# A hybrid encoder layer: gate-weighted one-hots and the forget gate move to ScalarE, one product of the expert search moves to VectorE in 16 bits, and the row fetches get a fifth slot and a wider spacing

## The chip, the core and the metric

The kernel runs on one core of one Trainium2 chip. The metric is the device time of one execution in microseconds (us). The engines are TensorE (PE in the profile; PEld is its weight load), VectorE (DVE), ScalarE (ACT), GpSimd (POOL) and SyncE (SP), each with a queue of its own that runs in order; 16 DMA engines move data between HBM and SBUF.

## What is computed

One layer over 1024 tokens of width 1024: a mixer, and a feed-forward part that picks single-neuron experts.

```python
h    = rmsnorm(x, norm_mix_g)
proj = h @ w_in                                   # q, forget, i, out gate, conv B/C/h, two merge gates
forget = lb + (1 - lb) * sigmoid(hf);  k = 1 - forget;  log_f = log(forget)
y_a  = gated_norm(hgrn2_chunkwise(q, k, log_f, i)) # recurrence in chunks of 64 tokens, 8 heads
y_b  = cb * causal_depthwise_conv(cc * ch, conv_w)
x    = x + (sig(g_a) * (y_a @ w_branch_hg) + sig(g_b) * (y_b @ w_branch_conv)) @ w_out
# experts: 8 heads, 128 x 128 product keys, 16 picks a head
h2   = rmsnorm(x, norm_ffn_g)
s1, s2 = scores of the 128 first and the 128 second keys;  top 16 of each
top_s, pos = top_k(v1[:, None] + v2[None, :], 16);  idx = cand_i[pos];  gate = softmax(top_s)
x    = x + sum over the 128 picks of gate * gelu(peer_u[idx] . h2) * peer_v[idx]
out  = rmsnorm(x, norm_final_g)
```

## The kernel before

The 1024 tokens are 8 tiles of 128. The kernel has two stages.

The **mixer stage** works through five groups of tokens (128, 128, 256, 256, 256). For a group, `front` normalizes and transposes, `recurrence` (L554) makes the gates and runs the chunks, `gates_b` and `gates_a` make the merge gates, and `post` (L603) multiplies by the branch and output matrices, adds the residual, normalizes again and finds the top 16 keys of each head. `picks_of` then runs `pick` (L817) for each tile: 50 candidate sums a head, their top 16, and the number of the expert behind each. For that last step a head compares 16 positions with 50 candidate places on VectorE (L860, 16 x 50 = 800 elements), multiplies the result with the candidates' numbers on GpSimd (L862) and sums on VectorE (L863).

What is done with the picks depends on the tile. Tiles 0, 1, 6 and 7 go **by rows** (`gather`, L895): for each of a token's 128 picks an indirect DMA of GpSimd (L905) fetches one 4 KB row of table U per token, VectorE multiplies it with h2 and sums (L935); 32 picks later the same is done with the rows of table V (L941, into the output). The rows lie in a ring of slots; a slot is fetched anew when the product that reads it is done. Tiles 2 to 5 go **densely**: `all_gates` (L960) writes, for each token, a 128 x 128 table of gates to HBM (the tile wd), and the second stage applies all 16384 experts to those 512 tokens. For the gates, keys and gates of a tile are transposed on PE (L881) and copied out (L887, L889, L890); then, 8 tokens at a time, VectorE makes one-hots of both keys (L998) and multiplies one of them by the gate, in an upper and a lower half of 16 bits (L1002); PE multiplies the two (L979) and ScalarE copies the result out (L983). There are 64 such steps of 8 tokens, 16 a tile.

The **dense stage** (`dense`, L1013) begins when the gates are complete: per block of 128 experts it splits weights into two halves (L238), projects (L286, L289), applies gelu (L1031) and the gates (L1033), and multiplies with V (L1058, L1069). Rows of tiles 6 and 7, and the picks of these tiles, are laid between its steps by `interleave` (L415). At the end come the sums with the residual (L1117) and the final norms.

The order of the mixer stage is set by a planner, `together` (L386). It keeps a clock of PE work, takes of all running pieces the one that is least far behind its budget, and lets it run to its next `yield`; a number that is yielded is a pause on that clock. `PICK` is the pause between the end of a search and the transposes of its keys, `SPREAD` that between making one-hots and multiplying them, and `ROW_STEP` that between two row steps in `paced` (L372); a row step is two rows of U and two of V. Tiles 0 and 1 need 136 row steps. Each engine then works in this order, as a scheduler of the framework puts it.

## Time and profile before

| | us |
|---|---|
| median of 3 runs (lowest, highest) | 3249.61 (3244.61, 3250.73) |
| the profiled execution | 3238.13 |
| its span, first to last instruction | 3236.4 |
| busy: PE / DVE / ACT / POOL | 2830.8 / 2677.1 / 1075.6 / 1577.1 |
| DMA | 979.05 MB, mean 303 GB/s |
| mean granted TensorE clock | 0.927 of full speed |

The mixer stage fills the span up to about 1790 us, the dense stage from there to about 3190; the final 49 us hold norms and the last rows. Busy shares are averages over these stages and say little by themselves. A wait is put down to what ended it last.

### The profile page before, as it was taken

Reading aid. Unit: us, or ns where it says so; the run is one execution under the profiler, and the core shown is the slowest. Engines: PE = TensorE matmul, PEld = TensorE weight load, DVE = VectorE, ACT = ScalarE, POOL = GpSimd, SP = SyncE. Lnnn points to the kernel's source line nnn. Section 1 sums busy time; section 2 is a strip of 40 time slices with the busy share of each in tenths; the row PEclk is TensorE's granted clock in tenths of the full one; section 3 lists DMA queues with packets and bytes.
Section 4 is the critical chain, followed back from the end, with each engine's and each line's share of the span. In section 5 each row is a group of like instructions: output and inputs, shape, how many; then the busy total and the mean of one; then the engine's idle time right before and its main releaser. Section 6 shows DMA issues by size and latency. Waiting matters only on the chain.

```text
span 3236.4 us, 45285 instructions
## 1 busy us (share of the span) xinstructions
PE 2830.8 (87%) x15988; PEld 2434.0 (75%) x15988; DVE 2677.1 (83%) x5673; ACT 1075.6 (33%) x1686; POOL 1577.1 (49%) x1392
## 2 busy tenths in 40 slices
...
GB/s 284 190 273 242 270 316 321 318 273 331 316 305 306 237 288 310 324 299 276 292 304 264 257 283 344 340 351 312 355 314 349 315 355 324 349 319 343 330 328 195
DMA packets 336131, 979.05 MB, mean 303 GB/s; under 512 B 30880, under 2 KB 107168, under 8 KB 333856
## 3 DMA queue, kind: packets, MB, share of 16 engines
...
q8 instruction: 126, 2.06, 0.2%
q14 instruction: 101, 0.83, 0.1%
...
## 4 chain that ended last, share of the span: by engine, by line
PE 56%; DVE 23%; DMA 9%; issue 5%; ACT 3%; POOL 3%; SPq 0%; DVEq 0%; POOLq 0%; ACTq 0%
PE ps L1058 15%; PE ps L286 14%; PE ps L250 10%; PE ps L289 7%; DVE mem_g L941 5%; DMA mem_g<-in_peer_u,idx 4%; DVE mem_g L935 4%; DMA mem_g<-in_peer_v,idx 4%; PE ps L277 2%; PE ps L278 2%; PE ps L279 2%; PE ps L736 1%; DMA mem_z<-in_keys 1%; DVE mem_z L863 1%; DVE mem_y L1002 1%
## 5 line engine op out<-in xcount | busy, mean ns | idle before, releaser
L250 PE MATMUL ps<-mem_h,mem_w 128*128 128x256 f32 (+1 forms) x4480 | 856.8, 350 | 10.4 <-ACT mem_h L260 8.7
L250 PEld LDWEIGHTS ps<-mem_h,mem_w 128*128 128x128 f32 x4480 | 743.4, 200 | 88.0 <-ACT mem_h L260 10.2
L905 POOL DMA_INDIRECT mem_g<-in_peer_u,idx x384 | 486.6, 1267 | 503.6 <-DVE mem_g L935 305.1
L905 POOL DMA_INDIRECT mem_g<-in_peer_v,idx x368 | 450.8, 1225 | 442.2 <-DVE mem_g L941 202.2
L1058 PE MATMUL ps<-mem_v,mem_ph 128*128 128x512 f32 x2304 | 552.2, 390 | 0.5 <-ACT mem_v L237 0.5
L941 DVE SCALAR_TENSOR_TENSOR mem_g<-mem_g 128x1024 f32<-128x1024 f32 x368 | 494.9, 1345 | 50.3 <-DMA mem_g<-in_peer_v,idx 50.0
L935 DVE SCALAR_TENSOR_TENSOR mem_g<-mem_g 128x1024 f32<-128x1024 f32 x384 | 487.1, 1272 | 38.4 <-DMA mem_g<-in_peer_u,idx 37.6
L286 PE MATMUL ps<-mem_ht,mem_s 128*128 128x512 f32 x2048 | 510.6, 392 | 7.0 <-DVE mem_z L1069 4.3
L1058 PEld LDWEIGHTS ps<-mem_v,mem_ph 128*128 128x128 f32 x2304 | 432.6, 188 | 90.4 <-ACT mem_v L237 0.9
L286 PEld LDWEIGHTS ps<-mem_ht,mem_s 128*128 128x128 f32 x2048 | 387.0, 189 | 88.9 <-DVE mem_z L1069 4.9
L237 ACT ACTIVATE mem_s<-mem_raw 128x512 fp32r<-128x512 f32 x256 | 161.2, 631 | 573.3 <-PE ps L286 559.0
L905 POOL DMA_INDIRECT mem_e<-in_peer_u,idx x128 | 186.4, 1456 | 220.9 <-DVE mem_e L935 192.4
L289 PE MATMUL ps<-mem_ht,mem_s 128*128 128x512 f32 x1024 | 275.2, 391 | 0.0
L238 DVE TENSOR_TENSOR mem_s<-mem_raw,mem_s 128x512 fp32r<-128x512 f32 x256 | 177.1, 700 | 110.1 <-PE ps L289 73.2
L905 POOL DMA_INDIRECT mem_e<-in_peer_v,idx x144 | 173.3, 1203 | 139.9 <-DVE mem_g L941 94.0
L289 PEld LDWEIGHTS ps<-mem_ht,mem_s 128*128 128x128 f32 x1024 | 193.4, 189 | 40.3
L941 DVE SCALAR_TENSOR_TENSOR mem_g<-mem_e,mem_g 128x1024 f32<-128x1024 f32 x144 | 184.3, 1280 | 1.3 <-DMA mem_g<-x2d 1.1
L237 ACT ACTIVATE mem_v<-mem_z 128x1024 fp32r<-128x1024 f32 x128 | 128.9, 1053 | 156.7 <-PE ps L279 156.3
L701 POOL TENSOR_TENSOR mem_y<-mem_y 128x128 f32<-128x128 f32 (+1 forms) x120 | 60.1, 501 | 233.4 <-DVE mem_y L570 233.3
L983 ACT COPY mem_a<-ps 128x512 f32<-128x512 f32 x128 | 124.3, 1086 | 140.2 <-PE ps L979 71.2
L862 POOL TENSOR_TENSOR mem_z<-mem_z 128x800 f32<-128x800 f16 x64 | 125.2, 1956 | 86.7 <-DVE mem_z L860 76.0
L935 DVE SCALAR_TENSOR_TENSOR mem_e<-mem_e,mem_g 128x1024 f32<-128x1024 f32 x128 | 156.7, 1230 | 1.5 <-DMA mem_e<-in_peer_u,idx 1.5
(189 smaller groups left out, 3975.9 us busy)
## 6 DMA issues: line engine op xcount, KB each, us to landing
mem_w<-in_w_in SPq DMA_DIRECT2D x200, 512.0 KB, 5.3
mem_raw<-in_peer_ut SPq DMA_DIRECT2D x128, 512.0 KB, 6.8
mem_z<-in_peer_v SPq DMA_DIRECT2D x128, 512.0 KB, 7.8
...
```

The source lines that it names most:

```text
L237: self.nc.scalar.activation(hi, src, AF.Copy)
L238: self.nc.vector.tensor_tensor(lo, src, hi.bitcast(F32), op=ALU.subtract)
L250: self.nc.tensor.matmul(ps, w[:, kk, :], act[:, kk, :], start=kk == 0, stop=kk == k - 1)
L277: mm(ps, lh, rh, start=first, stop=False, **kw)
L286: mm(ps, w[kk][0], act[part][:, kk, :], start=kk == part == 0, stop=False)
L289: mm(ps, w[j][1], act[0][:, j, :], start=False, stop=j == k - 1)
L862: nc.gpsimd.tensor_tensor(pr, eq, ci[:, hd:hd + 1, :].broadcast_to([P, TOPK, NCAND]), op=ALU.mult)
L905: nc.gpsimd.indirect_dma_start(out=r, out_offset=None, in_=a[table], in_offset=bass.IndirectOffsetOnAxis(ap=self.idx[t][:, k:k + 1], axis=0))
L935: nc.vector.scalar_tensor_tensor(u, u, 1.0, h2, op0=ALU.mult, op1=ALU.mult, accum_out=wt[:, k:k + 1])
L941: nc.vector.scalar_tensor_tensor(acc, v, wt[:, k:k + 1], acc, op0=ALU.mult, op1=ALU.add)
L983: nc.scalar.copy(dst[:, :, 4 * h:4 * h + 4].rearrange("p a t -> p t a"), ps.rearrange("p (t a) -> p t a", t=4))
L1058: nc.tensor.matmul(acc[t][hf], pp[c][i][:, tk], vp[c][:, k, 512 * hf:512 * hf + 512], start=c == 0 and i == 0 and k == 0, stop=c == NKEYS ...
```

## The change

Four edits, and three numbers of the planner.

- `all_gates`: the product of the one-hot with the gate leaves VectorE. In place of one instruction of 2048 elements (L1002) ScalarE does 16 activations of 128 elements, each with the token's gate half as its scale, one value per partition. The gate halves are kept as [2, 128] in 32 bits for it, so `pick` copies them out in another way (one more copy on ScalarE, a narrower subtraction on VectorE). The one-hots have two buffers and not three.
- `recurrence`: forget = lb + (1 - lb) * sigmoid and k = 1 - forget leave VectorE (L567, L568) and become two activations with scale and bias.
- `pick`: the product with the candidates' numbers (L862) leaves GpSimd for VectorE; one-hot, numbers and product are unsigned 16-bit integers, which takes one more cast of 400 elements a tile.
- The ring of row slots in the mixer stage has five slots of 4 KB (the fifth is the buffer that the one-hots gave up). The dense stage has eight, as before.
- `ROW_STEP` 6.2 to 7.0, `PICK` 31.25 to 50, `SPREAD` 1.296 to 2.592.

```diff
@@ constants @@
-T_SOON, T_ROWS, ROW_STEP = 300.0, 1e4, 6.2
+T_SOON, T_ROWS, ROW_STEP = 300.0, 1e4, 7.0
...
-LEV, GRAM, STATE, MERGE, NORM, PICK, SPREAD, OUT = 11.55, 1.944, 0.864, 4.752, 3.24, 31.25, 1.296, 3.24
+LEV, GRAM, STATE, MERGE, NORM, PICK, SPREAD, OUT = 11.55, 1.944, 0.864, 4.752, 3.24, 50.0, 2.592, 3.24
@@ place, place_picks, place_dense, schedule @@
-        M.o, M.q = r((80, 84, 220), 4), r((56, 60), 4)
+        M.o, M.q = r((80, 84), 4), r((56, 60), 4)
...
-        M.pr, M.fi, M.ci = r(at + 4, 3.25), r(at + 4, 1), r(at + 7.25, 1.625)
+        M.pr, M.cu, M.fi, M.ci = r(at + 4, 1.625), r(at + 5.625, 1), r(at + 4, 1), r(at + 7.25, 1.625)
...
-        M.rows = (80, 84, 216, 220)
+        M.rows = (80, 84, 216)
...
-        self.rows = self.ring(300, 4, 4)
+        self.rows = self.ring((300, 304, 308, 312, 220), 4)
@@ constants() @@
+        self.one = c.tile([P, 1], F32, tag="one", name="one")
+        nc.vector.memset(self.one, 1.0)
@@ recurrence @@
             nc.scalar.activation(fg, fp[:, :n], AF.Sigmoid)
-            nc.vector.tensor_scalar(fg, fg, self.oml[:, p:p + 1], self.lb[:, p:p + 1], op0=ALU.mult, op1=ALU.add)
-            nc.vector.tensor_scalar(k, fg, -1.0, 1.0, op0=ALU.mult, op1=ALU.add)
+            nc.scalar.activation(fg, fg, AF.Identity, bias=self.lb[:, p:p + 1], scale=self.oml[:, p:p + 1])
+            nc.scalar.activation(k, fg, AF.Identity, bias=self.one, scale=-1.0)
             nc.scalar.activation(fg, fg, AF.Ln)
@@ pick @@
+        cu = mem.cu.take([HEADS, NCAND], U16)
+        nc.vector.tensor_copy(cu, ci)
...
         for hd in range(HEADS):
-            eq, pr = mem.eq.take([TOPK, NCAND], F16), mem.pr.take([TOPK, NCAND])
+            eq, pr = mem.eq.take([TOPK, NCAND], U16), mem.pr.take([TOPK, NCAND], U16)
             nc.vector.tensor_tensor(eq.rearrange("p k (c d) -> p k c d", d=2), ix,
                                     pf[:, hd].unsqueeze(2).broadcast_to([P, TOPK, NCAND // 2, 2]), op=ALU.is_equal)
-            nc.gpsimd.tensor_tensor(pr, eq, ci[:, hd:hd + 1, :].broadcast_to([P, TOPK, NCAND]), op=ALU.mult)
+            nc.vector.tensor_tensor(pr, eq, cu[:, hd:hd + 1, :].broadcast_to([P, TOPK, NCAND]), op=ALU.mult)
             nc.vector.tensor_reduce(xf[:, hd, :], pr, axis=AX.X, op=ALU.add)
...
-        pairs = ps[:, 2 * P:3 * P].unsqueeze(2).broadcast_to([P, P, 2])
-        nc.scalar.copy(gates[:, :, 0, :], pairs)
-        nc.vector.tensor_tensor(gates[:, :, 1, :], pairs, gates[:, :, 0, :], op=ALU.subtract)
+        upper = self.small.tile([P, P], F16, tag="upper", name="upper", bufs=1)
+        nc.scalar.copy(upper, ps[:, 2 * P:3 * P])
+        nc.scalar.copy(gates[:, 0], ps[:, 2 * P:3 * P])
+        nc.vector.tensor_tensor(gates[:, 1], ps[:, 2 * P:3 * P], upper, op=ALU.subtract)
@@ all_gates @@
                     nc.vector.tensor_tensor(o.rearrange("p t i (k d) -> p (t i) k d", d=2), ix,
                                             keys.rearrange("p t i d -> p (t i) d").unsqueeze(2)
                                             .broadcast_to([P, 2 * T, NKEYS // 2, 2]), op=ALU.is_equal)
-                    first = o[:, :, 1, :].rearrange("p t (k d) -> p t k d", d=2)
-                    nc.vector.tensor_tensor(q.rearrange("p t i (k d) -> p t i k d", d=2),
-                                            first.unsqueeze(2).broadcast_to([P, T, 2, NKEYS // 2, 2]),
-                                            gates.unsqueeze(3).broadcast_to([P, T, 2, NKEYS // 2, 2]), op=ALU.mult)
                     yield SPREAD if todo else 0
+                    for tk in range(T):
+                        for i in range(2):
+                            nc.scalar.activation(q[:, tk, i, :], o[:, tk, 1, :], AF.Copy, scale=gates[:, i, tk:tk + 1])
```

How the order of the engines moves at three places. Line numbers of the change are higher by 3 to 7.

PE before, where the last group's recurrence ends: L250 with `mem_yy` is the branch product of `post`, L881 the transposes of tile 4's keys, L979 the one-hot products.

```order
L765 MATMUL ps<-mem_y 64x64 x4
L784 MATMUL ps<-mem_y,c_headmean 128x256
L250 MATMUL ps<-mem_h_157,mem_w 128x256 x32
L250 MATMUL ps<-mem_yy,mem_w 128x256 x32
L881 MATMUL ps<-c_ident,mem_z 128x128 x3
L979 LDWEIGHTS mem_o
L979 MATMUL ps<-mem_y,mem_o 128x128
```

PE with the change, at the same place (L886 are the transposes, L632 is the output projection of `post`, L629 before):

```order
L768 MATMUL ps<-mem_y 64x64 x4
L787 MATMUL ps<-mem_y,c_headmean 128x256
L251 MATMUL ps<-mem_h_159,mem_w 128x256 x32
L251 MATMUL ps<-mem_yy,mem_w 128x256 x32
L632 MATMUL ps<-mem_w,mem_h_159 128x256 x32
L886 MATMUL ps<-c_ident,mem_z 128x128 x3
L986 LDWEIGHTS mem_o
L986 MATMUL ps<-mem_y,mem_o 128x128
```

All 32 products of the first half of the output projection have moved ahead of the transposes.

ScalarE before, from the copies of tile 4's keys and gates on (L887, L889): L983 copies tables of gates out, L847 is the exponential of tile 5's gates, L230 the square sum of the last group's second norm.

```order
L887 CAST mem_z<-ps 128x128x2 x2
L889 CAST mem_z<-ps 128x128x2
L983 COPY mem_a<-ps 128x4x128 x2
L847 ACT_TABLE_LOAD
L847 ACTIVATE mem_z<-mem_z 128x128
L983 COPY mem_a<-ps 128x4x128 x8
L230 ACTIVATE junk,ms<-mem_z 128x1024
L983 COPY mem_a<-ps 128x4x128 x2
L230 ACTIVATE junk,ms<-mem_z 128x1024
```

ScalarE with the change, right behind the copies of tile 4's keys and gates (L990 copies tables out, L850 is the exponential, L231 the square sum, L1012 are the new activations):

```order
L990 COPY mem_a<-ps 128x4x128 x2
L850 ACT_TABLE_LOAD
L850 ACTIVATE mem_z<-mem_z 128x128
L1012 ACTIVATE mem_y<-mem_o,mem_z 128x128 x37
L990 COPY mem_a<-ps 128x4x128 x2
L1012 ACTIVATE mem_y<-mem_o,mem_z 128x128 x11
L990 COPY mem_a<-ps 128x4x128 x2
L231 ACTIVATE junk,ms<-mem_z 128x1024
L990 COPY mem_a<-ps 128x4x128
L1012 ACTIVATE mem_y<-mem_o,mem_z 128x128 x16
L990 COPY mem_a<-ps 128x4x128
L231 ACTIVATE junk,ms<-mem_z 128x1024
```

The two square sums now stand behind 48 and 64 of the new activations.

VectorE before, one head of tile 4's search (L860 compares, L863 sums; between them GpSimd multiplies; L611 is the branch product's gating in `post`):

```order
L863 TENSOR_REDUCE mem_z<-mem_z 128x16
L860 TENSOR_TENSOR mem_z<-iota_x,mem_z 128x800
L935 SCALAR_TENSOR_TENSOR mem_g<-mem_g 128x1024
L611 TENSOR_TENSOR mem_z<-mem_z,ps 128x256
L941 SCALAR_TENSOR_TENSOR mem_g<-mem_g 128x1024
L611 TENSOR_TENSOR mem_z<-mem_z,ps 128x256
L935 SCALAR_TENSOR_TENSOR mem_g<-mem_g 128x1024
L863 TENSOR_REDUCE mem_z<-mem_z 128x16
```

VectorE with the change, one head of the same search (L865 compares, L867 multiplies, L868 sums; L942 and L948 are row products, `mem_a` holds the fifth slot):

```order
L868 TENSOR_REDUCE mem_z<-mem_z 128x16
L865 TENSOR_TENSOR mem_z<-iota_x,mem_z 128x800
L948 SCALAR_TENSOR_TENSOR mem_g<-mem_a,mem_g 128x1024
L867 TENSOR_TENSOR mem_z<-mem_z 128x800
L942 SCALAR_TENSOR_TENSOR mem_g<-mem_g 128x1024
L868 TENSOR_REDUCE mem_z<-mem_z 128x16
```

The product stands between compare and sum on the same engine.

## Rows read from the trace of the kernel before

**Rows 1.** The windows of the profiled execution, by stretch: start and end in us from the span's start, length, then busy us (instructions) of each engine, the granted clock of TensorE as a share of full speed, the busy share of the DMA engines, and GB/s. Picks stand for the search of each token's 128 experts; tiles 2 and 3 are searched from about 1000, tiles 4 and 5 from about 1450, tiles 6 and 7 from about 1750.

```profile
300.00:1050.00 750.00, 665.43 (x4190) 584.54 (x4188) 599.96 (x1589) 233.60 (x404) 388.36 (x415) 0.92 0.87 308
1050.00:1512.00 462.00, 352.93 (x2361) 306.27 (x2361) 421.91 (x1060) 171.74 (x251) 256.38 (x221) 0.87 0.81 285
1512.00:1600.00 88.00, 38.80 (x227) 33.77 (x227) 81.81 (x133) 17.57 (x23) 53.66 (x36) 0.69 0.83 296
1600.00:1800.00 200.00, 125.71 (x848) 111.38 (x849) 190.39 (x511) 77.51 (x111) 100.85 (x69) 0.76 0.85 298
1800.00:3188.00 1388.00, 1383.27 (x6090) 1144.91 (x6090) 1206.01 (x1692) 442.86 (x648) 723.32 (x541) 1.00 0.90 323
3188.00:3237.00 49.00, 2.49 (x11) 1.71 (x10) 42.48 (x89) 5.75 (x10) 15.95 (x14) 0.55 0.58 214
```

**Rows 2.** Who waited for whom from 1050 to 1800: engine, tile and line that waited, what it waited for, us in total, times, longest.

```profile
PE ps L881 <- DVE mem_z L877: 131.3, 4, 48.0
PE ps L979 <- DVE mem_y L1002: 69.0, 13, 21.0
```

**Rows 3.** The timeline of PE around the key transposes of tiles 4 and 5: start us, length us, instruction, and in brackets the idle time before it and what ended it.

```profile
1451.13 12.79 PE L250 MATMUL ps<-mem_yy,mem_w 128*128 128x256 f32 x58 [0.55 <-DVE mem_yy L796]
1511.96 0.90 PE L881 MATMUL ps<-c_ident,mem_z 128*128 128x128 f32 x3 [48.04 <-DVE mem_z L877]
...
1600.25 0.88 PE L881 MATMUL ps<-c_ident,mem_z 128*128 128x128 f32 x3 [45.67 <-DVE mem_z L877]
```

**Rows 4.** Groups of VectorE up to 1870 us, one shape each: line, operation, output<-input, shapes, count | busy us, mean ns of one | idle us before them and what ended it. The picture of what the change takes off VectorE and of the nearest relatives of what it puts there.

```profile
L1002 DVE TENSOR_TENSOR mem_y<-mem_o,mem_z 128x2048 f16<-128x2048 f16 x43 | 57.0, 1327 | 0.5 <-PE ps L979 0.4
L1002 DVE TENSOR_TENSOR mem_y<-mem_a,mem_z 128x2048 f16<-128x2048 f16 x21 | 26.0, 1237 | 0.0
L567 DVE TENSOR_SCALAR mem_y<-mem_y,oml,lb 128x256 f32<-128x256 f32 x12 | 6.4, 531 | 1.8 <-ACT mem_y L566 1.8
L567 DVE TENSOR_SCALAR mem_y<-mem_y,oml,lb 128x128 f32<-128x128 f32 x8 | 2.8, 346 | 4.0 <-ACT mem_y L566 4.0
L568 DVE TENSOR_SCALAR mem_y<-mem_y 128x256 f32<-128x256 f32 x12 | 3.5, 290 | 0.1
L568 DVE TENSOR_SCALAR mem_y<-mem_y 128x128 f32<-128x128 f32 x8 | 1.8, 222 | 0.1
L860 DVE TENSOR_TENSOR mem_z<-iota_x,mem_z 128x800 f16<-128x800 f16 x64 | 36.4, 569 | 0.0
L863 DVE TENSOR_REDUCE mem_z<-mem_z 128x16 f32<-128x800 f32 x63 | 61.5, 976 | 12.7 <-POOL mem_z L862 12.6
```

**Rows 5.** The row products of VectorE (L935 with the row of table U, L941 with that of V), same columns: two groups up to 1870 us, two groups from 1870 us on, and two from 1448 to 1512 us, where tile 4 is searched.

```profile
L935 DVE SCALAR_TENSOR_TENSOR mem_g<-mem_g 128x1024 f32<-128x1024 f32 x256 | 331.9, 1299 | 38.3 <-DMA mem_g<-in_peer_u,idx 37.6
L941 DVE SCALAR_TENSOR_TENSOR mem_g<-mem_g 128x1024 f32<-128x1024 f32 x224 | 310.5, 1386 | 50.1 <-DMA mem_g<-in_peer_v,idx 50.0
...
L941 DVE SCALAR_TENSOR_TENSOR mem_g<-mem_g 128x1024 f32<-128x1024 f32 x144 | 184.4, 1281 | 0.2
L935 DVE SCALAR_TENSOR_TENSOR mem_e<-mem_e,mem_g 128x1024 f32<-128x1024 f32 x128 | 156.7, 1230 | 1.5 <-DMA mem_e<-in_peer_u,idx 1.5
...
L941 DVE SCALAR_TENSOR_TENSOR mem_g<-mem_g 128x1024 f32<-128x1024 f32 x11 | 19.3, 1758 | 2.4 <-DMA mem_g<-in_peer_v,idx 2.4
L935 DVE SCALAR_TENSOR_TENSOR mem_g<-mem_g 128x1024 f32<-128x1024 f32 x11 | 18.3, 1662 | 2.6 <-DMA mem_g<-in_peer_u,idx 2.6
```

**Rows 6.** The product of the search on GpSimd up to 1870 us, same columns.

```profile
L862 POOL TENSOR_TENSOR mem_z<-mem_z 128x800 f32<-128x800 f16 x63 | 123.2, 1955 | 84.6 <-DVE mem_z L860 74.0 <-DVE rs_t L219 4.6 <-DVE mem_y L754 3.3
```

**Rows 7.** The timeline of VectorE and GpSimd in the search of tile 4.

```profile
1493.09 1.27 DVE L941 SCALAR_TENSOR_TENSOR mem_g<-mem_g 128x1024 f32<-128x1024 f32 x1
1494.00 1.85 POOL L862 TENSOR_TENSOR mem_z<-mem_z 128x800 f32<-128x800 f16 x1
1494.29 2.64 DVE L935 SCALAR_TENSOR_TENSOR mem_g<-mem_g 128x1024 f32<-128x1024 f32 x1
```

**Rows 8.** Groups of ScalarE up to 1870 us, one shape each, same columns.

```profile
L983 ACT COPY mem_a<-ps 128x512 f32<-128x512 f32 x128 | 124.3, 1086 | 140.2 <-PE ps L979 71.2 <-DMA wd<-mem_a 57.0 <-DVE mem_g L935 11.1
L517 ACT ACTIVATE mem_a<-mem_a,c_convw 128x256 f32<-128x256 f32 x12 | 6.1, 507 | 92.0 <-DVE mem_a L512 91.9
L517 ACT ACTIVATE mem_a<-mem_a,c_convw 128x128 f32<-128x128 f32 x8 | 3.2, 401 | 12.5 <-DVE mem_a L512 12.5
L789 ACT ACTIVATE mem_y<-mem_y 128x128 f32<-128x128 f32 x8 | 2.5, 309 | 0.3
L569 ACT ACTIVATE mem_y<-mem_y 128x256 f32<-128x256 f32 x12 | 5.0, 417 | 16.3 <-DVE mem_y L568 16.3
```

**Rows 9.** The timeline of ScalarE at two activations that follow each other without a wait.

```profile
1224.73 0.42 ACT L708 ACTIVATE mem_y<-mem_y 128x256 f32<-128x256 f32 x1
1225.05 0.19 ACT L710 ACTIVATE el<-mem_y 128x4 f32<-128x4 f32 x1
```

**Rows 10.** The timeline of VectorE at the end: the last sum with a PSUM bank, the first and the last two of the 22 row products that follow it, and the last instruction.

```profile
3187.12 1.28 DVE L1069 TENSOR_TENSOR mem_z<-mem_z,ps 128x512 f32<-128x512 f32 x2 [4.03 <-PE ps L279]
...
3196.38 1.28 DVE L941 SCALAR_TENSOR_TENSOR mem_g<-mem_g 128x1024 f32<-128x1024 f32 x1
...
3225.17 2.61 DVE L941 SCALAR_TENSOR_TENSOR mem_g<-mem_e,mem_g 128x1024 f32<-128x1024 f32 x2
...
3231.18 1.28 DVE L956 SCALAR_TENSOR_TENSOR mem_g<-mem_g,rstd,mem_e 128x1024 f32<-128x1024 f32 x1
```

More of the change, by code (lines that the diff above doesn't have):

```diff
@@ L15 @@
 I32 = mybir.dt.int32
+U16 = mybir.dt.uint16
 U32 = mybir.dt.uint32
@@ L46 @@
 NCAND = int(sum(NB))
-ITEM = {F32: 4, F32R: 4, U32: 4, I32: 4, F16: 2, BF16: 2}
+ITEM = {F32: 4, F32R: 4, U32: 4, I32: 4, U16: 2, F16: 2, BF16: 2}
 ALWAYS = {"z": (112, 163.5), "g": (300, 325)}
```

8 lines of the change are left out of this document (5 added, 3 removed).

## The prediction, on record before the change was run

> **What bounds the kernel now.** I read the windows by stretch first [rows 1]. From 1800 to 3188 us PE is busy 1383 of 1388 us at a granted clock of 1.00 while VectorE is busy 87%: that stage is PE's. From 1600 to 1800 VectorE is busy 190 of 200 us and PE 126; from 1050 to 1600 VectorE is busy 504 of 550 us (422 and 82) and PE 392. These two stretches are VectorE's, although PE has the larger share over the whole span. From 300 to 1050 nobody is: PE 665, VectorE 600 of 750, the DMA engines at 87%. ScalarE is busy 38% (172, 18 and 78 of 750 us) from 1050 to 1800. Then the waits: PE waits 131.3 us in four waits for the keys of the dense tiles, and 69.0 us for the gate-weighted one-hots [rows 2]; the timeline shows two of the former, 48.04 and 45.67 us, with PE's queue behind them [rows 3]. While PE waits there VectorE works, so such a wait is mostly a sign of VectorE's backlog, and only worth what VectorE can do sooner. At the end, the last PSUM sums start at 3187, and 22 products with V rows run from 3196 to 3228 with the last norms between them [rows 10].
>
> **What VectorE loses and gains.** The gate products take 57.0 + 26.0 = 83.0 us in 64 instructions, the forget gate 6.4 + 2.8 + 3.5 + 1.8 = 14.5 us in 40 [rows 4]. Both go. What comes is 64 products of 800 elements. No row shows one in unsigned 16 bits; nearest is the comparison L860, two 16-bit inputs and as many elements, at 569 ns: 36.4 us. The upper end is the sum L863, which reads 800 elements in 976 ns: 62.5 us. Eight casts of 400 elements lie between L568's 290 ns and L860's 569: about 0.42 each, 3.4 us. The narrower subtraction of the gates is worth under 1 us. Net **-58 us** (-32 if the product is slow).
>
> To this come stalls. In the search of tile 4 the row products take 1758 and 1662 ns, in the dense stage 1281 and 1230 [rows 5]: 11 x 0.48 + 11 x 0.43 = 10 us lost beside the 8 products that GpSimd makes there, so 1.25 us a product in row products alone. The timeline shows one: alone L941 takes 1.27 us; an L935 that starts at 1494.29, 0.29 us after a GpSimd product of 1.85, takes 2.64 and ends 1.1 us after it [rows 7]. Bounds are 0 and the whole 1.955 us of a product [rows 6]; I take 1.0, nearer to the counted rows: **64 us** over all tiles. By the Trainium skill's page "SBUF — State Buffer" (SBUF: two separate sides) a GpSimd operation and a VectorE one with two SBUF inputs lock each other out of a port pair for the whole instruction; the row agrees in kind, and by that page VectorE would get back 125 us, not 64. VectorE's own waits for GpSimd's product, 12.6 us [rows 4], go too.
>
> Row products: the wider step moves none out of the mixer stage (254 and 219 stand ahead of the first dense gating before, 256 and 224 now), only later in it. Ahead of tile 2's keys stand 255 before and 233 now; ahead of tile 5's, 414 and 401; behind those, up to the dense stage, 59 and 79.
>
> **What ScalarE gains.** 1024 activations of 128 elements with a scale read per partition. Nearest is L517 of that shape: 401 ns, against 309 for L789 without such a scale [rows 8]. Neighbours that need not wait overlap: L710 starts at 1225.05, L708 ends at 1225.15 [rows 9]. So 0.30 us from start to start, 307 us in all; the ends are 0.21 (309 less the overlap) and 0.40 (no overlap), 215 and 410. The forget gate adds 12 x 2 x 0.507 + 8 x 2 x 0.401 = 18.6 us by L517's rows; in return ScalarE no longer waits 16.3 us for L568 [rows 8].
>
> **Stretch by stretch**, against the profiled execution of 3238.1 us (span 3236.4), which lies 11.5 under the median of the runs.
>
> - 300 to 1050: 22 row products fewer (27 us) and some 12 us of forget gates less; 24 heads of products more (13.7), 24 us of stalls less: VectorE -49. PE and DMA are near their own ends here, so I take a third: **-15**, with 0 and -45 as ends.
> - 1050 to 1600: 39 gate products less (50 us), 3 of forget gates; 24 heads more (13.7), 24 us of stalls and some 8 of the 12.6 of waits less; 9 row products more (11). VectorE -60 of 504. But ScalarE goes from 189 to about 400 us: 672 activations (204), six table copies more. In a stretch of under 500 us that is over 80%, in order. Half the projection is now ahead of tile 4's transposes on PE, which helps; both square sums of the last norm stand behind 48 to 64 activations on ScalarE, which hurts. I take about 60%: **-37**, ends +15 and -65.
> - 1600 to 1800: 25 gate products less (32 us) and 6 us of stalls; 20 row products more (25) and 8 heads (4.6): VectorE -8. ScalarE: 352 activations (106) more, six table copies (6.5) less, 78 to 177 us of 200. **0**, ends +25 and -15.
> - 1800 to 3188: PE's, the same instructions: **0**.
> - The end: fewer idle row steps (135 steps are placed in the mixer stage, all of use; 139 before, three of which found no picks) leave 14 row products behind the last PSUM sum, not 22. 31.4 us for 22 with the norms between [rows 10] is 1.4 each; 8 fewer is 11, less a little for norms without cover: **-10**.
>
> Sum -62: the profiled execution would be 3176, the median 3249.6 - 62 = **3188 us**. This case takes in 3155 to 3220.
>
> **Rivals.**
>
> 1. *ScalarE's queue becomes the pace* (slower). In the new order the activations stand in 93 blocks, and behind 59 of them something other than a table copy follows directly: a step of the recurrence, a query's copy, a norm. A block of 16 is 4.8 us and itself waits for its one-hot from VectorE, with two buffers in place of three. At half a block each, 59 waits are 142 us; half of it on the path, 71 us, takes the place of the 37 gained from 1050 to 1600: 3249.6 - 25 + 34 = 3259. It decides once waits on the path exceed 62 us. For it: 400 us of work in under 500; 0.40 a piece would make that 465. Against it: ScalarE idled most of the stretch [rows 1]. The Trainium skill's page "ScalarE: Activation LUTs" (Rules for kernel authors) says to multiply on VectorE and not on ScalarE, and speaks against this edit; here the engine that it would spare is the one with time left. Chance 0.15.
> 2. *The relief is not passed on.* PE, the DMA engines or row fetches fill what VectorE leaves; rows already cost it 37.6 + 50.0 us of waits [rows 5]. Only the end's 10 us show: 3240. Against: VectorE was busy 95% ahead of the dense stage. Chance 0.15.
> 3. *All of it counts.* -45, -65, -15 and -10: 3115. It needs ScalarE to be nowhere late. Chance 0.10.
> 4. *The product does not run at 16-bit speed*, 976 ns and not 569: 26 us back, some 16 of them on the path: 3204. Chance 0.10.
>
> The forecast keeps 0.50. Range **3135 to 3262**: it takes in the forecast, rivals 2 and 4, half of rival 1 and part of rival 3; left out are the far ends of 1 and 3. A measurement of this kernel tells some 0.2% (6.5 us) from no change. Faster by more: 0.50 + 0.10 + 0.10 and over half of rival 2, 0.78; within it: the rest of rival 2, 0.07; slower: rival 1, 0.15.
>
> **What would show it.** Right: L941 and L935 near 1281 and 1230 ns in the searches; the stretch in which PE is always busy beginning some 50 us earlier than 1800; PE's waits for the keys well under 131 us; the new activations about 0.30 apart; 14 row products at the end. Wrong: VectorE idle for ScalarE between 1050 and 1800, a product near 976 ns, or an unmoved start of the dense stage.

## The result: 0.8% faster, where 1.9% was forecast

The changed kernel takes **3224.74 us**, the median of 4 runs (3220.0 to 3228.39), the kernel before 3250.17 beside it: ratio 0.9919, 95% interval 0.9893 to 0.9946. That is 25 us less, outside what measurement can take for no change; the forecast was 62 less. Its profiled execution took 3228.39 us, with a span of 3226.6. One run of the experiment e13 below, at 4212.51 us and a granted clock of 0.642, is left out of its median.

Lines have moved: the product is now L867, the comparison L865, the sum L868, the new activations L1012, the one-hot products on PE L986, the key transposes L886, the row products L942 (table U) and L948 (table V), the dense V products L1065 and L278 to L280 (before L1058 and L277 to L279).

The windows after, over the stretches of [rows 1]:

```profile
300.00:1050.00 750.00, 680.28 (x4226) 596.27 (x4225) 567.65 (x1656) 249.24 (x429) 364.16 (x386) 0.92 0.83 300
...
1050.00:1512.00 462.00, 381.58 (x2393) 319.54 (x2392) 386.16 (x975) 307.97 (x765) 226.50 (x220) 0.88 0.85 309
1512.00:1600.00 88.00, 64.03 (x394) 52.03 (x393) 81.16 (x194) 75.51 (x213) 38.13 (x30) 0.83 0.90 328
...
1600.00:1800.00 200.00, 142.16 (x679) 96.31 (x678) 178.61 (x549) 171.40 (x453) 83.69 (x64) 0.72 0.83 296
1800.00:3188.00 1388.00, 1388.00 (x6029) 1130.37 (x6028) 1178.77 (x1591) 433.49 (x633) 704.04 (x530) 1.00 0.88 320
...
3188.00:3237.00 49.00, 1.43 (x7) 0.81 (x5) 32.65 (x79) 5.04 (x10) 7.67 (x6) 0.64 0.35 129
```

From 1050 to 1600 VectorE (the third pair) is busy 36 us less (467 against 504; the forecast had 60 less) and ScalarE (the fourth) 194 more (the forecast had some 210). PE is busy all of 1800 to 3188, as before, and yet does not get through: it runs 6029 instructions where it ran 6090.

The groups of VectorE up to 1870 us and over the whole span (the 16-bit ones), and the new one of ScalarE:

```profile
L942 DVE SCALAR_TENSOR_TENSOR mem_g<-mem_g 128x1024 f32<-128x1024 f32 x206 | 257.2, 1252 | 25.4 <-DMA mem_g<-in_peer_u,idx 23.1 <-issue 1.7
L948 DVE SCALAR_TENSOR_TENSOR mem_g<-mem_g 128x1024 f32<-128x1024 f32 x183 | 239.2, 1307 | 22.6 <-DMA mem_g<-in_peer_v,idx 22.3
...
L868 DVE TENSOR_REDUCE mem_z<-mem_z 128x16 f32<-128x800 uint16 x64 | 62.6, 979 | 0.3
L867 DVE TENSOR_TENSOR mem_z<-mem_z 128x800 uint16<-128x800 uint16 x64 | 37.9, 592 | 0.2
...
L1012 ACT ACTIVATE mem_y<-mem_o,mem_z 128x128 f16<-128x128 f16 x1024 | 309.2, 398 | 22.1 <-DVE mem_o L1006 22.1
```

Against [rows 4, 5]: the product costs 592 ns, the sum no longer waits for GpSimd (0.3 us, not 12.7), and the row products fell from 1299 and 1386 ns to 1252 and 1307. The activations take 309 us for 1024, 0.30 us each.

Who waited for whom from 1050 to 1800:

```profile
PE ps L986 <- ACT mem_y L1012: 46.3, 17, 6.6
ACT mem_z L892 <- PE ps L886: 34.5, 1, 34.5
...
ACT mem_y L1012 <- DVE mem_o L1006: 22.1, 12, 3.9
```

PE's 131.3 us of waits for the keys [rows 2] are gone from this list (the timeline has one left, 14.27 us, at tile 4's); PE now waits for ScalarE. That the key waits are gone is not by itself a sign of a lighter VectorE: e10, told below, has VectorE's gate products and the old `PICK`, and 77.0 us of them; e16, with `PICK` at 50 as in the change, 13.5. First e10, then e16:

```profile
PE ps L884 <- DVE mem_z L880: 77.0, 3, 33.5
...
PE ps L886 <- DVE mem_z L882: 13.5, 1, 13.5
```

The same marks in the traces give the stretches (us; a mark is the start of that work; those that begin with e are experiments told below, e6 being a second profile of the kernel before):

| stretch | before | e6 | after | e3 | e4 | e8 | e9 | e10 | e17 | e16 |
|---|---|---|---|---|---|---|---|---|---|---|
| start to keys of tile 2 | 1062.9 | 1055.9 | 1048.8 | 1071.6 | 1036.7 | 1072.2 | 1045.0 | 1028.9 | 1035.5 | 1045.0 |
| keys of tile 2 to keys of tile 5 | 537.3 | 545.7 | 545.6 | 524.1 | 524.5 | 552.5 | 553.9 | 537.7 | 541.7 | 547.4 |
| keys of tile 5 to first dense projection | 183.4 | 186.6 | 172.8 | 189.3 | 179.6 | 169.4 | 189.6 | 188.3 | 188.5 | 172.1 |
| first projection to last V product | 1406.5 | 1405.8 | 1421.8 | 1396.0 | 1407.3 | 1401.5 | 1405.0 | 1399.5 | 1399.5 | 1397.7 |
| last V product to last norm | 41.1 | 41.1 | 32.5 | 41.7 | 32.5 | 51.9 | 21.9 | 21.9 | 22.0 | 32.5 |

Two profiles of the same kernel differ by up to 8 us in a stretch of the mixer stage and by under 1 us in the dense stage; so a difference of a few us in the first three lines is not read as one. The experiments e1, e5, e13 and e16 run the change's instructions in its order on every engine, e2 those of the kernel before; over these five profiles of the change the first three lines average 1046.8, 546.9 and 172.3 us, over the three of before 1061.2, 543.5 and 185.0. The profiled executions differ by 9.7 us, the medians by 25: the one of before was 12 under its median, that of after 4 over.

### The profile page after: what moved, and what is told of

It is laid out like the page before. It is cut to its first block, busy times and chain, and to the rows that moved or that the text cites. A ratio compares the mean times of both kernels' runs of the same rounds, so it can differ in the third digit from the quotient of the medians.

```text
span 3226.6 us, 46082 instructions
## 1 busy us (share of the span) xinstructions
PE 2920.7 (91%) x15988; PEld 2447.9 (76%) x15988; DVE 2558.0 (79%) x5642; ACT 1374.8 (43%) x2748; POOL 1451.9 (45%) x1328
## 4 chain that ended last, share of the span: by engine, by line
PE 50%; DVE 12%; ACT 11%; DMA 5%; issue 3%; POOL 2%; DVEq 0%; ACTq 0%; POOLq 0%; SPq 0%
PE ps L1065 17%; PE ps L287 14%; PE ps L290 7%; ACT mem_y L1012 6%; PE ps L251 3%; DVE mem_g L948 3%; ACT mem_a L990 3%; DVE mem_g L942 2%; PE ps L278 2%; PE ps L279 2%; PE ps L280 2%; DMA wd<-mem_a 2%; DMA mem_g<-in_peer_v,idx 1%; DMA mem_g<-in_peer_u,idx 1%; PE ps L739 1%
## 5 line engine op out<-in xcount | busy, mean ns | idle before, releaser
L251 PE MATMUL ps<-mem_h,mem_w 128*128 128x256 f32 (+1 forms) x4480 | 869.5, 353 | 21.3 <-ACT mem_h L261 10.0
L912 POOL DMA_INDIRECT mem_g<-in_peer_u,idx x332 | 410.8, 1237 | 422.2 <-DVE mem_g L942 123.3
L912 POOL DMA_INDIRECT mem_g<-in_peer_v,idx x324 | 396.2, 1223 | 426.4 <-DVE mem_g L942 217.4
L1065 PE MATMUL ps<-mem_v,mem_ph 128*128 128x512 f32 x2304 | 569.2, 396 | 3.2 <-ACT mem_ph L238 3.2
L1065 PEld LDWEIGHTS ps<-mem_v,mem_ph 128*128 128x128 f32 x2304 | 433.4, 188 | 109.4 <-ACT mem_ph L238 3.6
L287 PE MATMUL ps<-mem_ht,mem_s 128*128 128x512 f32 x2048 | 507.4, 390 | 1.0 <-DVE mem_ht L239 0.9
L287 PEld LDWEIGHTS ps<-mem_ht,mem_s 128*128 128x128 f32 x2048 | 384.5, 188 | 83.5 <-DVE mem_ht L239 1.3
L948 DVE SCALAR_TENSOR_TENSOR mem_g<-mem_g 128x1024 f32<-128x1024 f32 x324 | 419.6, 1295 | 26.5 <-DMA mem_g<-in_peer_v,idx 25.7
L942 DVE SCALAR_TENSOR_TENSOR mem_g<-mem_g 128x1024 f32<-128x1024 f32 x332 | 410.1, 1240 | 28.5 <-DMA mem_g<-in_peer_u,idx 26.2
L912 POOL DMA_INDIRECT mem_e<-in_peer_u,idx x128 | 189.6, 1482 | 324.3 <-DVE mem_e L942 284.0
L1012 ACT ACTIVATE mem_y<-mem_o,mem_z 128x128 f16<-128x128 f16 x1024 | 309.2, 398 | 22.1 <-DVE mem_o L1006 22.1
L290 PE MATMUL ps<-mem_ht,mem_s 128*128 128x512 f32 x1024 | 274.0, 390 | 0.0
L290 PEld LDWEIGHTS ps<-mem_ht,mem_s 128*128 128x128 f32 x1024 | 192.2, 188 | 40.1
L986 PE MATMUL ps<-mem_y,mem_o 128*128 128x128 f16 x1024 | 135.4, 243 | 65.2 <-ACT mem_y L1012 46.3
L948 DVE SCALAR_TENSOR_TENSOR mem_g<-mem_e,mem_g 128x1024 f32<-128x1024 f32 x144 | 184.3, 1280 | 2.9 <-DMA mem_g<-x2d 2.6
L986 PEld LDWEIGHTS <-mem_o 128*128 128x128 f16 x1024 | 82.9, 106 | 115.8 <-issue 93.6
```

The costliest lines, as they stand in the source:

```text
L251: self.nc.tensor.matmul(ps, w[:, kk, :], act[:, kk, :], start=kk == 0, stop=kk == k - 1)
L287: mm(ps, w[kk][0], act[part][:, kk, :], start=kk == part == 0, stop=False)
L290: mm(ps, w[j][1], act[0][:, j, :], start=False, stop=j == k - 1)
L912: nc.gpsimd.indirect_dma_start(out=r, out_offset=None, in_=a[table], in_offset=bass.IndirectOffsetOnAxis(ap=self.idx[t][:, k:k + 1], axis=0))
L942: nc.vector.scalar_tensor_tensor(u, u, 1.0, h2, op0=ALU.mult, op1=ALU.mult, accum_out=wt[:, k:k + 1])
L948: nc.vector.scalar_tensor_tensor(acc, v, wt[:, k:k + 1], acc, op0=ALU.mult, op1=ALU.add)
```

## The experiments

Each was run in 5 rounds beside the kernel before (median 3248 to 3251 us throughout), but for e6. Intervals are 95%.

**Why is the dense stage longer?** In the trace after, successive V products start 234 ns apart (median), in the one before 227; the projections (L287, L290) stay at 227. There are 3072 of them, and the groups of PE show what it costs. Before, then after, then e16 of below:

```profile
L1058 PE MATMUL ps<-mem_v,mem_ph 128*128 128x512 f32 x2304 | 552.2, 390 | 0.5 <-ACT mem_v L237 0.5
...
L278 PE MATMUL ps<-mem_v,mem_ph 128*128 128x512 f32 x256 | 99.7, 390 | 0.0
```
```profile
L1065 PE MATMUL ps<-mem_v,mem_ph 128*128 128x512 f32 x2304 | 569.2, 396 | 3.2 <-ACT mem_ph L238 3.2
...
L279 PE MATMUL ps<-mem_v,mem_ph 128*128 128x512 f32 x256 | 101.1, 395 | 0.0
```
```profile
L1065 PE MATMUL ps<-mem_v,mem_ph 128*128 128x512 f32 x2304 | 551.5, 389 | 0.0
...
L278 PE MATMUL ps<-mem_v,mem_ph 128*128 128x512 f32 x256 | 99.6, 389 | 0.0
```

17 us on the 2304 products and 1.4 on each of three groups of 256: 21 us. PE runs the same 6144 dense products there, in an order that differs in some places; what differs besides is that the new tiles `one` (32 bytes) and `upper` (256) push mem_v up by 288 bytes in SBUF, while mem_ph stays. Theory A: this place is the cause. e1 enlarges `one` so that mem_v is another 32 bytes higher, e2 shifts the kernel before by 288 bytes, with no instruction changed:

```diff
-        self.one = c.tile([P, 1], F32, tag="one", name="one")
+        self.one = c.tile([P, 16], F32, tag="one", name="one")[:, 0:1]
```
```diff
-        self.eps = c.tile([P, 1], F32, tag="eps", name="eps")
+        self.eps = c.tile([P, 80], F32, tag="eps", name="eps")[:, 0:1]
```

> The changed kernel with one constant made 32 bytes longer, so that all tiles on the left side of SBUF start at 32 modulo 64 bytes, as in the kernel before (in the change they start at 0 modulo 64); the order of every engine is that of the change. Theory A (place in SBUF): the 3072 V products of the dense stage go back from 234 ns apart to 227, 21 us; the kernel takes about 3203 us. Rival B (that execution was slow on PE by chance, or the change of order slows PE): they stay at 234 ns or vary from run to run, and the time stays at 3225.

> The kernel before with one constant made 288 bytes longer, so that its left-side tiles start where those of the change do (0 modulo 64); same order on every engine. Theory A: its V products go from 227 to 234 ns and it takes 21 us more, about 3271. Rival B: no difference, 3250.

e1: 3203.06 us, ratio 0.9858 (0.9833 to 0.9883), 229 ns. e2: 3271.84, ratio 1.0066 (1.0041 to 1.0091), 234 ns: a kernel made 23 us slower by 288 bytes that nobody uses. Is it the place of mem_v, or its place against mem_ph? e5 leaves mem_v and moves mem_ph 32 bytes down:

```diff
-            "e1": (216, 224), "ph": (200, 216)}
+            "e1": (216, 224.03125), "ph": (200, 216)}
```

> The changed kernel, same instructions in the same order, with the right-hand region that holds mem_ph started 31.97 bytes on, so that mem_ph too starts at 0 modulo 64 bytes, as mem_v does in the changed kernel. Theory F (what counts is how the two operands of a V product lie to each other): V products back from 234 to 227 ns from start to start, the dense stage about 1404 us, time about 3203 us, ratio 0.986. Rival G (what counts is the place of mem_v by itself, at 0 and not at 32 modulo 64): V products stay at 234 ns, time about 3225 us, ratio 0.992.

3210.6 us (0.9855 to 0.9908) and 229 ns, not 227: moving mem_ph alone helps, so it is the distance; but neither e1 nor e5 is quite back. I took the distance modulo 128 bytes for the rule and tried it with `[P, 32]` in the place of `[P, 16]` in e1, e12 and e11:

> The changed kernel once more, same order, with the tile one of 128 bytes, so that mem_v starts at 96 modulo 128 bytes like mem_ph, as in the kernel before. So far the V products were 227 ns apart where mem_v and mem_ph have the same start modulo 128 (before, e3, e9, e10), 229 where they differ by 64 (e1, e4, e5, e7, e8, e11, e12), 234 where they differ by 32 (after, e2). If that is what counts: 227 ns here and 3072 x 2.3 ns = 7 us less than e1, about 3196 us. Rival: 229 ns comes of the changed code and not of the place, 3203 us.

> e12_forget_on_scalar with the tile one of 128 bytes (mem_v at 96 modulo 128). Theory: of the 17 us that e12 lost against e10, 7 were the place: 227 ns, about 3198 us, and the 10 left are the forget gate's. Rival: the place is not it, 3205 us.

> e11_half_step_7_8 with mem_v at 96 modulo 128: V products at 227 ns, 7 us less than its 3182, about 3175 us. Rival: 3182 us.

That rule fell at once: 232.5 ns, and 3219.23, 3220.12 and 3195.17 us, each 14 to 16 slower. Read modulo 256 all runs agree, and `[P, 64]` in e1, e12 and e11 puts it to the test:

> The changed kernel, same order, with the tile one of 256 bytes, so that the distance from mem_v to mem_ph is 0 modulo 256 bytes, as in the kernel before. The rule by 128 bytes fell with e13 to e15 (232 ns at a distance of 128 modulo 256). By the runs so far the V products are 227 ns apart at 0 modulo 256 (before, e3, e9, e10), 229 at 192, 232 at 128, 234 at 224. Theory: 227 ns here, dense stage 6 to 7 us shorter than in e1, 3196 us (3190 to 3202). Rival: only the old absolute place gives 227 ns, or another residue counts; 229 ns or more and 3203 us or more.

> e10_rows_and_product with the forget gate on ScalarE and the distance from mem_v to mem_ph at 0 modulo 256 bytes as in e10. Theory: 227 ns; of e12's 17 us over e10 some 7 were the place, so 3198 us, and 10 us are the forget gate's move, through the order. Rival: nearly all 17 were the place, 3188 us.

> e11_half_step_7_8 (half of the gate products on ScalarE, row step 7.8) at 0 modulo 256. Theory: 7 us less than e11's 3182, about 3175 us; rival: 3182 us or more.

226.7 ns in all three. e16: 3200.87 us, ratio 0.9859 (0.9833 to 0.9885); e17: 3194.12 (0.9817 to 0.9859); e18: 3181.3 (0.9772 to 0.9806).

| distance mem_v to mem_ph, modulo 256 bytes | V products apart (mean of steps under 0.3 us, ns) | kernels |
|---|---|---|
| 0 | 226.7 | before, e3, e6, e9, e10, e16, e17, e18 |
| 192 | 228.9 | e1, e4, e5, e7, e8, e11, e12 |
| 128 | 232.5 | e13, e14, e15 |
| 224 | 233.3 | after, e2 |

The edits give these distances as shifts against the kernel before, whose own the expectations put at 0; no trace shows an address. Kernels whose shifts differ by 256 agree: 64 and 320 bytes (e12, e1), 128 and 384 (e14, e13), 0, 256 and 512 (before, e17, e16).

So the place costs the changed kernel 24 us (after against e16); in the two profiles the stretch from the first dense projection to the last V product differs by 24.1. The times are less regular than the ns: e16 was to come out 7 us below e1 and came out 2 below, and e18 level with e11, with intervals that reach as far as the difference expected.

**What is each part worth?** e3 is the product on VectorE in 16 bits alone (with the change's tiles and cast for it), e9 the rows alone (the slot at 220 taken from the one-hots and the dense stage as in the change), e10 both. Of e3 the product's line, of e9 the two lines that name its numbers:

```diff
...
-            nc.gpsimd.tensor_tensor(pr, eq, ci[:, hd:hd + 1, :].broadcast_to([P, TOPK, NCAND]), op=ALU.mult)
+            nc.vector.tensor_tensor(pr, eq, cu[:, hd:hd + 1, :].broadcast_to([P, TOPK, NCAND]), op=ALU.mult)
```
```diff
...
-T_SOON, T_ROWS, ROW_STEP = 300.0, 1e4, 6.2
+T_SOON, T_ROWS, ROW_STEP = 300.0, 1e4, 7.0
...
-        self.rows = self.ring(300, 4, 4)
+        self.rows = self.ring((300, 304, 308, 312, 220), 4)
```

> The kernel before with one part of the change alone: the product of the search in 16 bits on VectorE. Tiles stay where they were. Theory C (GpSimd's products stalled VectorE): VectorE loses about 64 us of stalls and 12 of waits for 40 us of new work, the row products of the searches fall from 1758 and 1662 ns to near 1281 and 1230, and the dense stage starts some 15 to 25 us earlier: about 3230. Rival: the stalls were only shifted to other GpSimd work and the time stays within 6 us of 3250.

> The kernel before with the change's part on rows alone: ROW_STEP 7.0, the fifth slot for rows in the place of the third one-hot buffer; gate products on VectorE, pick products on GpSimd as before. e8_row_step_6_2 lost 41 us by going back to 6.2. Theory H (the spacing is a gain by itself): most of that shows here, 3215 to 3230 us. Rival J (the wider spacing is worth something only once VectorE is lighter; in a full VectorE rows only fall in later places): within 10 us of 3250 us, the tail shorter by some 8 us and the mixer stage longer.

> e9_rows_only with the 16-bit pick product on VectorE too: the whole change but for what it moves to ScalarE (gate-weighted one-hots, forget gate). e3_product16_only alone gave 3227 us (-23). Theory K (ScalarE's part, 307 us of activations, gave nothing, since ScalarE's queue paced the middle of the mixer stage): 3195 to 3208 us, as e1_after_base32 (3203) or better. Rival L (ScalarE's part is worth the 20 us or more that the lighter VectorE promised): 3220 us or more.

e3: 3227.14 us (0.9905 to 0.9956). e9: 3222.61 (0.9906 to 0.9939), so theory H and not J. e10: **3187.8** (0.9802 to 0.9829), which is theory K: without anything moved to ScalarE, and with the `PICK` and `SPREAD` of the kernel before, the kernel is 37 us faster than the whole change. e8 takes the spacing out of e1 (`ROW_STEP` 6.2), e6 is the kernel before again, for a second profile (its stretches stand in the table):

> The changed kernel at the old places in SBUF (as e1_after_base32), with the row products spaced at 6.2 as before and not at the wider step. Theory H (the gain up to the keys of tile 2, some 20 us, and that of the tail, some 8 us, come from the row products that fall later): 10 to 25 us slower than e1, about 3213 to 3228 us. Rival I (they come from the lighter VectorE, and the spacing only shifts work): within 4 us of 3203 us.

> The kernel before once more, unchanged, for a second profile. Theory: V products at 227 ns as in the first; the first projection of the dense stage nearer to 1797 us, as in e2_before_base0 with the same order, than to the 1783.6 us of the first profile, whose execution was some 11 us faster than the median. Rival: it starts at 1784 us again, and then the mixer stage of e2 was longer because of the places in SBUF too.

e8: 3244.28 us (0.9973 to 1.0004), 41 slower than e1 and more than expected; without the spacing all the rest of the change, at that distance, is worth nothing that can be told. e6: one run, 3242.05 us; its dense stage starts at 1788, between the two values and nearer the first profile's.

**What did ScalarE's part bring?** e4 leaves the lower halves of the gates on VectorE (one product of 1024 elements a step) and gives ScalarE 8 activations a step instead of 16; e11 is e4 with `ROW_STEP` 7.8; e7 takes the forget gate back to VectorE in e1; e12 puts it on ScalarE in e10. e10, e12 and e17 have the `PICK` and `SPREAD` of the kernel before, e16 those of the change; no run has these two numbers alone. The edits of e4 (but for how the gate halves are kept) and of e7:

```diff
...
+                    nc.vector.tensor_tensor(q[:, :, 1, :].rearrange("p t (k d) -> p t k d", d=2),
+                                            o[:, :, 1, :].rearrange("p t (k d) -> p t k d", d=2),
+                                            low.unsqueeze(2).broadcast_to([P, T, NKEYS // 2, 2]), op=ALU.mult)
                     yield SPREAD if todo else 0
                     for tk in range(T):
-                        for i in range(2):
-                            nc.scalar.activation(q[:, tk, i, :], o[:, tk, 1, :], AF.Copy, scale=gates[:, i, tk:tk + 1])
+                        nc.scalar.activation(q[:, tk, 0, :], o[:, tk, 1, :], AF.Copy, scale=gates[:, tk:tk + 1])
```
```diff
-            nc.scalar.activation(fg, fg, AF.Identity, bias=self.lb[:, p:p + 1], scale=self.oml[:, p:p + 1])
-            nc.scalar.activation(k, fg, AF.Identity, bias=self.one, scale=-1.0)
+            nc.vector.tensor_scalar(fg, fg, self.oml[:, p:p + 1], self.lb[:, p:p + 1], op0=ALU.mult, op1=ALU.add)
+            nc.vector.tensor_scalar(k, fg, -1.0, 1.0, op0=ALU.mult, op1=ALU.add)
```

> The changed kernel with tiles at 32 modulo 64 bytes and half of the gate products back on VectorE: ScalarE makes the upper half (8 activations a step, not 16), VectorE the lower half in one instruction of 1024 elements. Theory D (ScalarE's queue sets the pace from 1100 to 1350 and from 1600 to 1750): ScalarE loses 154 us, VectorE gains about 40, the dense stage starts 15 to 30 us earlier than in the change, about 3185 with theory A's 21. Rival E (VectorE is the bound there still): the 40 us come back on VectorE and it is no faster than the change with its tiles moved, 3203, or slower.

> e4_half_on_scalar (3197 us) with the row products spaced at 7.8 and not 7.0. Theory H (rows that fall later relieve the stretch up to the keys of tile 2, where VectorE, DMA engines and PE are all near their ends): another 5 to 15 us faster. Rival: 7.0 is enough already, and rows pushed past the dense stage lengthen the tail: the same or up to 15 us slower.

> The changed kernel at the old places in SBUF (as e1_after_base32), with the forget gate of the state back on VectorE: ScalarE loses some 18.6 us of work over the mixer stage, VectorE gains some 14.5 us. Theory D (ScalarE's queue sets the pace of the middle of the mixer stage): no slower than e1 (3203 us), perhaps 3 to 10 us faster, since a step of ScalarE's chain is shorter. Rival E (VectorE's work still sets it): some 10 us slower, about 3213 us.

> e10_rows_and_product with the forget gate on ScalarE as in the change, at the old places in SBUF: the whole change without the gate-weighted one-hots on ScalarE. e7_forget_on_vector against e1_after_base32 put the forget gate's move at a gain of 8.6 us while ScalarE had 1024 activations more to do; if the edits add up, 3179 us here (3187.8 less 8.6). Rival: it was worth something only for the order it brought there, and is within 4 us of 3188 us here.

e4: 3197.44 us (0.981 to 0.9865); e11: 3181.58 (0.9793 to 0.9835); e7: 3211.68 (0.9866 to 0.9915); e12: 3204.97 (0.9829 to 0.9888). The forget gate on ScalarE is worth 9 us in one company (e7 to e1) and costs 6 in another (e10 to e17, both at distance 0), with intervals that overlap both times: presumably it acts through the order that the planner makes of it, and its own price isn't settled. The gate products on ScalarE together with the two raised pauses cost 7 us (e17 to e16), again with intervals that overlap. What the runs do show is that all of this together brought nothing: e16 is 13 us slower than e10, and the intervals of the two (0.9833 to 0.9885, 0.9802 to 0.9829) do not meet.

The two profiles are 18 us apart, and the table shows where: 16 ahead of tile 2's keys, 10 from there to tile 5's, 11 at the end, less 16 and 2 in the stretches between. Ahead of tile 2's keys no gate activation has run: e17 has 7 of the 16 with the forget gate alone, and the rest comes with the planner's order, the raised pauses in it. How much of the 13 us these pauses are was not tested.

The middle shows what became of the relief. From 1050 on, e10, then e16, then e4:

```profile
1050.00:1600.00 550.00, 412.87 (x2739) 359.85 (x2738) 503.00 (x1171) 197.85 (x290) 270.77 (x243) 0.85 0.86 307
1600.00:1800.00 200.00, 127.87 (x776) 110.03 (x775) 195.60 (x581) 74.11 (x104) 77.28 (x59) 0.76 0.78 276
```
```profile
1050.00:1600.00 550.00, 446.13 (x2781) 372.03 (x2782) 464.83 (x1169) 382.18 (x975) 268.56 (x249) 0.88 0.86 311
1600.00:1800.00 200.00, 141.51 (x692) 95.80 (x691) 180.73 (x549) 171.27 (x448) 81.34 (x63) 0.72 0.84 294
```
```profile
1050.00:1600.00 550.00, 442.63 (x2912) 381.62 (x2911) 500.52 (x1279) 302.21 (x671) 261.30 (x246) 0.89 0.88 317
```

VectorE is 503 us busy in e10 and 465 in e16, doing as many instructions (1171 and 1169): it was relieved, and stood idle for what it was relieved of. In e4, which has the pauses of the change and half the activations, it is busy 501 us again and does 1279. The timeline of PE after, near the end of the mixer stage, then that of ScalarE, shows the pace:

```profile
1700.61 4.61 PE L986 MATMUL ps<-mem_y,mem_o 128*128 128x128 f16 x16 [4.73 <-ACT mem_y L1012]
1706.08 4.65 PE L986 MATMUL ps<-mem_y,mem_o 128*128 128x128 f16 x16 [0.86 <-ACT mem_y L1012]
```
```profile
1700.12 4.79 ACT L1012 ACTIVATE mem_y<-mem_o,mem_z 128x128 f16<-128x128 f16 x16
1704.78 1.06 ACT L990 COPY mem_a<-ps 128x512 f32<-128x512 f32 x1
1705.62 4.79 ACT L1012 ACTIVATE mem_y<-mem_o,mem_z 128x128 f16<-128x128 f16 x16
```

Two groups of 16 such products in e10:

```profile
1644.28 1.05 PE L982 MATMUL ps<-mem_y,mem_o 128*128 128x128 f16 x16
...
1654.71 1.89 PE L982 MATMUL ps<-mem_y,mem_o 128*128 128x128 f16 x16 [5.42 <-DVE mem_y L1005]
```

Where PE reaches the products before ScalarE is through, each one waits for its own activation: 16 take 4.65 us and not 1.05 to 1.89, and PE's other work stands behind them. Summed over the products, PE's steps of under 0.4 us come to 121.6 us after and 71.1 in e10, 50 us more; the rest of PE's wait is the 46.3 above. e4, with half the activations, has 73.6, and its stretch from tile 2's keys to tile 5's is 524.5 us, against 545.6 to 547.4 in the five profiles with all of them; e11, e15 and e18, with a row step of 7.8 besides, have 518.0 to 520.8. By the medians e4 is only 6 us faster than e1, with intervals that overlap (its profiled execution was 10 under its median).

**A faster version.** e18 (half of the gate products on ScalarE, forget gate on ScalarE, the change's pauses, row step 7.8, distance 0) takes 3181.3 us, 2.1% under the kernel before and 43 us under the change. e10, the change less its ScalarE part and its two pauses, takes 3187.8; the intervals of the two just meet (0.9772 to 0.9806, 0.9802 to 0.9829).

## Why the prediction was wrong

Direction right, size wrong: -25 us for -62. By the medians of the runs, in steps that add to it within 2 us (kernel before 3248 to 3250):

| step | us |
|---|---|
| rows spaced wider, fifth slot (e9) | -26 |
| 16-bit product on VectorE (e9 to e10) | -35 |
| forget gate to ScalarE (e10 to e17) | +6 |
| gate products to ScalarE, `PICK` and `SPREAD` raised (e17 to e16) | +7 |
| mem_v at the change's own place (e16 to after) | +24 |

The total of the forecast is that of the first two alone (-61 for -62), by accident: it is put together otherwise.

- **VectorE's instructions: right.** The product takes 592 ns (569 taken), so rival 4 fell; the sum's waits are gone. Row products before 1870 us got 47 and 79 ns shorter, about 30 us over 256 and 224 of them; but e9, the spacing alone, has 26 and 49 ns of that. e3, the product alone, shows the stall beside GpSimd by itself: 1299 to 1236 and 1386 to 1297 ns, 36 us. In the change's search of tile 4 the row products take 1433 and 1349 ns, less than the 1758 and 1662 of [rows 5] and not yet the dense stage's:

```profile
L948 DVE SCALAR_TENSOR_TENSOR mem_g<-mem_g 128x1024 f32<-128x1024 f32 x9 | 12.9, 1433 | 0.0
L942 DVE SCALAR_TENSOR_TENSOR mem_g<-mem_g 128x1024 f32<-128x1024 f32 x8 | 10.8, 1349 | 0.0
```

  Other instructions of VectorE gained as well: taken over all that both kernels have ahead of 1600 us, shape by shape, and by the difference of the means times the count, they cost 66 us less in e3 and 55 less in the change (15 less in e9, 4 more in the second profile of the kernel before). The forecast took 1.0 us for each of the 48 products there, so the term held. The page "SBUF — State Buffer" of the Trainium skill (SBUF: two separate sides), by which the forecast put it at 125 us over all tiles (94 for these 48 products), agrees in kind and not in that size.
- **300 to 1050, -15: right in size, not in what gave it.** Keys of tile 2 come 14 us earlier, in the first profiles and in the averages. e9 has as much by the wider spacing alone (1045.0), and e8 (with the raised `PICK`) and e3, both at the old spacing, nothing (1072.2 and 1071.6, against 1061.2 on average before): the stalls and the forget gate, two of the terms, gave no time there by themselves. Beside the wider spacing the product does add to it (e10, 1028.9).
- **1050 to 1600, -37: the step that failed first, and by most.** From tile 2's keys to tile 5's it is +8 (0 against e6, +3 between the averages). VectorE's relief came in its instructions, and ScalarE's 0.30 us too; false was to say that VectorE's load turns into time while ScalarE goes to 80%. In the windows from 1150 to 1350 of the trace after, ScalarE (fourth) is busy 187 of 200 us and VectorE (third) 137:

```profile
1150.00:1200.00 50.00, 41.95 (x319) 34.86 (x318) 29.73 (x47) 45.72 (x118) 16.10 (x13) 1.00 0.91 345
1200.00:1250.00 50.00, 32.90 (x199) 26.13 (x199) 33.31 (x70) 49.75 (x123) 24.49 (x26) 0.70 0.67 237
1250.00:1300.00 50.00, 41.12 (x309) 36.40 (x310) 40.28 (x99) 43.87 (x117) 20.47 (x18) 0.82 0.94 357
1300.00:1350.00 50.00, 43.98 (x284) 36.64 (x283) 33.59 (x89) 47.41 (x116) 23.58 (x26) 0.90 0.76 280
```

  That is rival 1, in its place and by its mechanism, with one thing that it lacked: PE follows each activation singly, and so is held too. By the averages it took the 37 us away and 3 more, 40 of the 71 it had been given. That ScalarE's load is the cause is borne out by e4: half the activations, the same pauses, and the stretch is 22 us shorter, where profiles of one kernel differ by 8. The page "ScalarE: Activation LUTs" of the Trainium skill (Rules for kernel authors) was cited against this edit, and the traces agree: 16 activations take 4.79 us, where VectorE's one instruction took 1.24 to 1.33 [rows 4]. (ScalarE's 38% from 1050 to 1800 in the prediction is 36 by its own figures; no term hangs on it.)
- **1600 to 1800, 0: wrong by a little.** -11 (-14 against e6, -13 between the averages), although PE waits for ScalarE there too; e10 and e17 have none of it (188.3, 188.5), so it comes with the gate products off VectorE or with the raised pauses. By the averages the two stretches together come to -9, where -37 were forecast.
- **1800 to 3188, "PE's, the same instructions", 0: the second step that failed.** The same instructions need not take the same time. +15 by the marks: 24 for the place of mem_v, less some 9 that came with the product (e3 1396.0 and e10 1399.5, against 1406.5 before and 1405.0 in e9), presumably since the searches inside that stage no longer hold VectorE up. Neither was in the range's reasoning; no rival had it.
- **The end, -10: right.** 14 row products behind the last sum, not 22, and 8.6 us less:

```profile
3185.97 1.28 DVE L1076 TENSOR_TENSOR mem_z<-mem_z,ps 128x512 f32<-128x512 f32 x2 [4.29 <-PE ps L280]
...
3198.54 1.28 DVE L948 SCALAR_TENSOR_TENSOR mem_g<-mem_g 128x1024 f32<-128x1024 f32 x1
...
3221.46 1.28 DVE L963 SCALAR_TENSOR_TENSOR mem_g<-mem_g,rstd,mem_e 128x1024 f32<-128x1024 f32 x1
```

  In e9 and e10, which have the planner's pauses `SPREAD` and `PICK` of before, only 6 are left and the end is 19 us shorter, and so it is in e17 with the forget gate on ScalarE: with the gate products there, or the raised pauses, part of what the wider spacing wins is given back.
- **Rows.** I priced them at -10 and a part of -15 and thought the offload the larger half. It was the other way round: -26 for them alone, nothing for the offload.
- **Rival 2** (relief not passed on) describes the gate products, not the pick product. **Rival 3** (all counts) fell with the middle stretch.

What stays open: what in the chip makes a matmul slower at some distances; and how the 13 us from e10 to e16 divide between the forget gate, the gate products and the two pauses, since each also reorders the rest.
